# Two convolution layers: a depthwise sum in two halves, later weight splits, and shifted copies spread over three engines

## The chip, the cores and the metric

The kernel runs on one core of one Trainium2 chip. The metric is the device time of one execution in microseconds (us). The engines that matter are TensorE (PE in the profile, with its weight loads as PEld), VectorE (DVE), ScalarE (ACT), GpSimd (POOL) and the queue of SyncE (SP), which issues all the loads. Each engine works through its own instructions strictly in the order of the program, and waits for others at semaphores.

## The reference, cut to what matters

The program is a trunk of four layers on 256 tokens of width 1024. Layers 0 and 3 begin with a convolution mixer, layer 1 with attention, layer 2 with a gated MLP, and each is followed by a channel mixer (ConvFFN). Only the convolution mixer is changed:

```python
def conformer_conv(x, w_in, b_in, w_dw, b_dw, ln_g, ln_b, w_out, b_out):
    h = x @ w_in + b_in                       # 1024 -> 2048
    a, g = jnp.split(h, 2, axis=-1)
    h = a * jax.nn.sigmoid(g)
    h = causal_dwconv(h, w_dw, b_dw)          # 31 taps along the tokens, per channel
    h = jax.nn.silu(layer_norm(h, ln_g, ln_b))
    return h @ w_out + b_out
```

## The kernel before, in words

All matmuls that need accuracy are made of three: a float32 weight tile `raw` is split into a rounded part `whi` (ACT, L87) and the remainder `wlo` (DVE, L88), and so are the activations (`xT_h`, `xT_l`); L105 to L107 add high by high, high by low and low by high.

The 1024 channels of a convolution are worked in four pairs `pr` of two 128-channel halves `n`. For each pair there are these steps:

- `project(pr)`: the input projection of the pair, 96 matmuls of 256 columns into two PSUM banks.
- `glu`: a sigmoid of the gate on ACT (`sg`, L429), and on DVE the gated product `hp` (named `chp`, L430).
- `copies` inside `glu`: 16 copies, each of a block of 32 partitions of `hp` into `h4`, shifted by s tokens, so that four taps can be multiplied at once. Those of ACT are on L422, those of DVE on L424. Pairs 0 to 2 copy both halves at once (32 x 512); pair 3 copies each half by itself (32 x 256). POOL only clears the borders (L411, L413).
- `diagonals(pr)`: the tap weights as small diagonal blocks `dg` (DVE, L404).
- `rest(pr)`: the taps that don't fill a group of four, into `cv`: one on ACT (L446), the others on DVE (L448).
- `taps(pr)`: the groups of four taps as matmuls on PE (L461), then one DVE addition into `cv` (L464).
- `to_tokens(pr, t)`: transposes of `cv` to token-major PSUM banks `tm` (L469), from which `stats` (L475) and `normalise` (L478) make the layer norm. `turn_z` (L483) turns the result back, `activate` (L490, L101, L102) applies the SiLU, and `proj_rows` multiplies with the output weights `wout`, which come in four units `q` of two row blocks.

The order on PE is that in which the code is written. The order on the other engines is fixed when the program is built. The pools have four buffers each for `raw`, `whi`, `wlo` and for the ordinary PSUM banks (`mm`), two for `h4` and three for `hp` and `cv`. So `h4` of pair 2 uses the buffer of pair 0 again, and that of pair 3 the one of pair 1.

The layer's steps stand in the order of this code:

Of the kernel before, what the change touches and what calls it, by code (L numbers as in the profile page):

```python
# [12 lines left out]
AF = mybir.ActivationFunctionType  # L13
# [3 lines left out]
P = 128  # L17
D = 1024
T = 256
# [5 lines left out]
PAD = KW - 1  # L25
# [2 lines left out]
ALPHA = (2 * DEPTH) ** 0.25  # L28
EPS = 1e-5


GROUPS = ((6, 6, 7, 7), (6, 6, 6, 7))
ACT_COPIES = ((11, 16, 12, 9), (7, 15, 13, 8))
GMIN, GMAX = min(map(min, GROUPS)), max(map(max, GROUPS))


@with_exitstack
def trunk(ctx: ExitStack, tc: tile.TileContext, ins, out):
    nc = tc.nc
    pe, dve, act, pool = nc.tensor, nc.vector, nc.scalar, nc.gpsimd  # L40
# [16 lines left out]
    def bank():  # L57
        return mmp.tile([P, 512], F32, name="mm", tag="mm")

    def acc_bank(t, h):  # L60
        return accp.tile([P, 512], F32, name=f"acc{t}{h}", tag=f"acc{t}{h}")

    def accs():
        return [[acc_bank(t, h) for h in range(2)] for t in range(2)]

    order = {}
# [30 lines left out]
    def unit_rows(w, k0, parts=1):  # L97
        return halves(load(w[k0 * P:(k0 + 2) * P, :].rearrange("(k p) n -> p k n", p=P), 2, D), 2, D, parts)
# [264 lines left out]
    def conv(j, prm, lv, turn, nxt, w_first):  # L363


        with tc.tile_pool(name=f"conv{j}", bufs=2) as p:
            wout = ins["a_w_out"][j]
# [40 lines left out]
            def glu(pr, bks):  # L408

                hp = p.tile([P, 2, PAD + T], F32, name="chp", tag="chp", bufs=3)  # L410
                pool.memset(hp[:, :, 0:PAD], 0.0)  # L411
                h4 = p.tile([P, 2, 4, PAD + T], F32, name="h4", tag="h4")
                pool.memset(h4[:, :, :, 0:PAD], 0.0)  # L413
                last = {}

                def copies(a, b):
                    for r in range(4):
                        for s in range(4):
                            src, dst = hp[32 * r:32 * r + 32, a:b, PAD:], h4[32 * s:32 * s + 32, a:b, r, PAD - s:PAD - s + T]
                            i = 4 * r + s  # L420
                            if i * ACT_COPIES[j][pr] // 16 != (i + 1) * ACT_COPIES[j][pr] // 16:
                                last["act"] = act.activation(out=dst, in_=src, func=AF.Identity).ins  # L422
                            else:
                                last["dve"] = dve.tensor_copy(dst, src).ins  # L424

                for n in range(2):
                    c = 2 * pr + n
                    sg = p.tile([P, T], F32, name="sg", tag="sg")
                    act.activation(out=sg, in_=bks[n][:, :T], func=AF.Sigmoid, bias=b_in[:, 8 + c:9 + c])  # L429
                    dve.scalar_tensor_tensor(out=hp[:, n, PAD:], in0=bks[n][:, T:], scalar=b_in[:, c:c + 1], in1=sg, op0=ALU.add, op1=ALU.mult)  # L430
                    if pr == 3:
                        copies(n, n + 1)
                if pr < 3:
                    copies(0, 2)
                return hp, h4, last
# [14 lines left out]

            def taps(pr, t0=0, t1=T, ns=(0, 1)):
                if (pr, t0) not in sums:
                    sums[pr, t0] = bank().rearrange("p (n t) -> p n t", n=2)
                ps = sums[pr, t0][:, :, 0:t1 - t0]
                for n in ns:
                    for g in reversed(range(GROUPS[j][pr])):

                        first_g = g == GROUPS[j][pr] - 1
                        a = t0 if first_g else max(t0, PAD - 4 * g - 3)
                        for r in range(4):  # L460
                            pe.matmul(out=ps[32 * r:32 * r + 32, n, a - t0:], lhsT=dg[pr][:, 4 * n + r, g, :], rhs=h4[pr][:, n, r, 4 * g + a:4 * g + t1],  # L461
                                      start=first_g, stop=g == 0)
                y = cv[pr][:, ns[0]:ns[-1] + 1, t0:t1]
                dve.tensor_tensor(out=y, in0=ps[:, ns[0]:ns[-1] + 1, :], in1=y, op=ALU.add)  # L464
# [7 lines left out]

            def stats(t, h):
                with tc.issue_after(order["dve"]):
                    dve.bn_stats(out=st[t][:, h, :], in_=tm[t][h])  # L475

            def normalise(t, h, mv, rs):
                dve.tensor_scalar(out=z[t][:, h * 512:(h + 1) * 512], in0=tm[t][h], scalar1=mv[:, 0:1], scalar2=rs, op0=ALU.subtract, op1=ALU.mult)  # L478
# [19 lines left out]
            hp[0], h4[0], _ = glu(0, b0)  # L498
            cv[0] = rest(0, hp[0])
            b = project(1)  # L500
            tm = accs()
            dg[1] = diagonals(1)
            hp[1], h4[1], _ = glu(1, b)
            cv[1] = rest(1, hp[1])
            taps(0)
            b = project(2)
            for t in range(2):
                to_tokens(0, t)
            lv = lv()
            nxt = nxt()  # L510
            dg[2] = diagonals(2)
            hp[2], h4[2], _ = glu(2, b)
            taps(1)
            b = project(3)
            for t in range(2):
                to_tokens(1, t)
            dg[3] = diagonals(3)
            ws = [unit_rows(wout, 2 * q) for q in range(2)]
            hp[3], h4[3], last = glu(3, b)
            order.update(last)  # L520
            cv[2] = rest(2, hp[2])
            cv[3] = rest(3, hp[3])
            taps(2, 0, P)
            taps(2, P, T, (0,))
            for t in range(2):
                stats(t, 0)
            nxt = nxt()
            to_tokens(2, 0)
            taps(3, 0, P)
# [388 lines left out]
```

## Time and profile before

| | |
|---|---|
| time, median of 3 runs | 1332.46 us (1331.25 to 1336.53) |
| time of the profiled execution | 1332.35 us |
| its span | 1330.4 us |
| PE busy | 1297.1 us, 97% of the span |
| DVE busy | 1038.2 us, 78% |
| ACT busy | 782.2 us, 59% |
| POOL busy | 56.0 us, 4% |

The span is the time from the first to the last instruction in the trace; the other 1.95 us of the time lie around it. The two convolutions take up about the first 121 us of the span and the stretch from 1027 to 1135 us. A busy share of PE near 100% means that there is always a matmul under way, not that the array works at its peak.

### The profile page before, as it was taken

Reading aid. Unit: us, or ns where it says so; the run is one execution under the profiler, and the core shown is the slowest. Engines: PE = TensorE matmul, PEld = TensorE weight load, DVE = VectorE, ACT = ScalarE, POOL = GpSimd, SP = SyncE. Lnnn points to the kernel's source line nnn. Section 1 sums busy time; section 2 is a strip of 40 time slices with the busy share of each in tenths; the row PEclk is TensorE's granted clock in tenths of the full one; section 3 lists DMA queues with packets and bytes.
Section 4 is the critical chain, followed back from the end, with each engine's and each line's share of the span. In section 5 each row is a group of like instructions: output and inputs, shape, how many; then the busy total and the mean of one; then the engine's idle time right before and its main releaser. Section 6 shows DMA issues by size and latency. Waiting matters only on the chain.

```text
span 1330.4 us, 21217 instructions
## 1 busy us (share of the span) xinstructions
PE 1297.1 (97%) x8338; PEld 1111.3 (84%) x8338; DVE 1038.2 (78%) x1539; ACT 782.2 (59%) x1138; POOL 56.0 (4%) x251
## 2 busy tenths in 40 slices
PE   8979999999999999999999999999999989999997
PEld 8768888886997988886788888988888977988886
DVE  4968987776686987776779665997777986987776
ACT  4973766653674766662555443676662873666661
POOL 0000000001011000100000000000000000000000
PEclk9989999999999999999999999999999999999999
DMA  7713955553732765553867553665553732665530
GB/s 255 258 48 113 296 193 187 186 182 108 245 121 79 256 205 189 192 190 119 314 221 260 166 191 127 220 216 187 187 190 95 238 128 65 220 216 192 189 134 32
DMA packets 167937, 239.79 MB, mean 180 GB/s; under 512 B 7253, under 2 KB 135838, under 8 KB 167838
## 3 DMA queue, kind: packets, MB, share of 16 engines
q1 hardware_dynamic: 167838, 238.44, 54.2%
q8 instruction: 65, 1.06, 0.3%
q14 instruction: 34, 0.28, 0.1%
HBM read 237.38 MB, written 1.05 MB: 179 GB/s over the span
## 4 chain that ended last, share of the span: by engine, by line
PE 90%; ACT 3%; DVE 3%; DMA 1%; issue 1%; SPq 1%; POOL 0%; DVEq 0%; ACTq 0%; POOLq 0%
PE mm L224 26%; PE mm L225 13%; PE acc L107 9%; PE acc L105 9%; PE acc L106 9%; PE mm L107 5%; PE mm L105 4%; PE mm L106 4%; PE mm L232 4%; ACT h L422 2%; PE mm L461 2%; PE mm L242 2%; PE mm L823 1%; DVE cv L448 1%; PE acc L642 1%
## 5 line engine op out<-in xcount | busy, mean ns | idle before, releaser
L88 DVE TENSOR_TENSOR wlo<-raw,whi 128x2048 fp32r<-128x2048 f32 (+2 forms) x239 | 450.0, 1891 | 128.6 <-ACT whi L87 128.1
L224 PE MATMUL mm<-xT_s,whi 128*128 128x512 f32 x1472 | 516.6, 395 | 0.0
L87 ACT ACTIVATE whi<-raw 128x2048 fp32r<-128x2048 f32 (+2 forms) x239 | 377.3, 1593 | 138.2 <-PE mm L224 77.7
L225 PE MATMUL mm<-xT_s,wlo 128*128 128x256 f32 x1472 | 412.3, 280 | 0.0
L224 PEld LDWEIGHTS mm<-xT_s,whi 128*128 128x128 f32 x1472 | 275.9, 187 | 64.1
L225 PEld LDWEIGHTS mm<-xT_s,wlo 128*128 128x128 f32 x1472 | 277.9, 189 | 1.6
L286 DVE SCALAR_TENSOR_TENSOR y<-hp,prm,y 128x256 f32<-128x256 f32 x352 | 164.6, 479 | 32.2 <-ACT y L281 26.1
L281 ACT ACTIVATE y<-hp,prm 128x256 f32<-128x256 f32 x160 | 94.3, 593 | 109.8 <-DVE hp L280 109.3
L105 PE MATMUL acc<-whi,hh 128*128 128x512 f32 x352 | 139.6, 397 | 0.0
L107 PE MATMUL acc<-whi,hl 128*128 128x512 f32 x352 | 139.5, 396 | 0.0
L106 PE MATMUL acc<-wlo,hh 128*128 128x512 f32 x352 | 139.1, 395 | 0.0
L105 PE MATMUL mm<-xT_s,whi 128*128 128x256 f32 x360 | 103.9, 289 | 0.0
L107 PE MATMUL mm<-xT_s,wlo 128*128 128x256 f32 x360 | 101.9, 283 | 0.0
L106 PE MATMUL mm<-xT_s,whi 128*128 128x256 f32 x360 | 101.8, 283 | 0.0
L279 ACT ACTIVATE hp<-mm,prm 128x256 f32<-128x256 f32 x160 | 74.1, 464 | 13.4 <-PE mm L225 13.4
L107 PEld LDWEIGHTS acc<-whi,hl 128*128 128x128 f32 x352 | 66.1, 188 | 17.3 <-DVE hl L102 1.5
L105 PEld LDWEIGHTS acc<-whi,hh 128*128 128x128 f32 x352 | 66.1, 188 | 15.8
L106 PEld LDWEIGHTS acc<-wlo,hh 128*128 128x128 f32 x352 | 66.1, 188 | 14.2
L232 PE MATMUL mm<-xT,raw 128*128 128x128 f32 x608 | 71.1, 277 | 0.4 <-DMA raw<-in_a_w_in_dram 0.4
L232 PEld LDWEIGHTS mm<-xT,raw 128*128 128x128 f32 x608 | 70.3, 194 | 1.2 <-issue 0.8
L105 PEld LDWEIGHTS mm<-xT_s,whi 128*128 128x128 f32 x360 | 69.0, 192 | 1.6 <-issue 1.5
L107 PEld LDWEIGHTS mm<-xT_s,wlo 128*128 128x128 f32 x360 | 69.0, 192 | 0.2 <-DVE wlo L88 0.2
(162 smaller groups left out, 1665.4 us busy)
## 6 DMA issues: line engine op xcount, KB each, us to landing
raw<-in_f_w_up_dram SPq DMA_DIRECT2D x88, 1024.0 KB
raw<-in_f_w_down_dram SPq DMA_DIRECT2D x44, 1024.0 KB
raw<-in_c_w_in_dram SPq DMA_DIRECT2D x24, 1024.0 KB
raw<-in_a_w_in_dram SPq DMA_DIRECT2D x12, 1024.0 KB
raw<-in_b_w_qkv_dram SPq DMA_DIRECT2D x12, 1024.0 KB
raw<-in_c_w_out_dram SPq DMA_DIRECT2D x12, 1024.0 KB
raw<-in_a_w_out_dram SPq DMA_DIRECT2D x8, 1024.0 KB
raw<-in_b_w_o_dram SPq DMA_DIRECT2D x4, 1024.0 KB
```

What stands on the lines that cost most here:

```text
L87: act.activation(out=h, in_=r, func=AF.Identity)
L88: dve.tensor_tensor(out=l, in0=r, in1=h.bitcast(F32), op=ALU.subtract)
L105: pe.matmul(out=ps, lhsT=lh, rhs=rh, start=start, stop=False)
L106: pe.matmul(out=ps, lhsT=lh, rhs=rl, start=False, stop=False)
L107: pe.matmul(out=ps, lhsT=ll, rhs=rh, start=False, stop=stop)
L224: pe.matmul(out=ps, lhsT=wh[:, k, n * P:(n + 1) * P], rhs=xT_hl[:, :, k, :], start=k == 0, stop=False)
L225: pe.matmul(out=ps[:, :T], lhsT=wl[:, k, n * P:(n + 1) * P], rhs=xT_h[:, :, k, :], start=False, stop=k == KT - 1)
L232: pe.matmul(out=ps[:, t * P:(t + 1) * P], lhsT=w[:, k, n * P:(n + 1) * P], rhs=xT[:, t, k, :], start=k == 0, stop=k == KT - 1)
L242: pe.matmul(out=ps, lhsT=xT[:, t, k, :], rhs=ws[k // 4][:, k % 4, :], start=k == 0, stop=k == KT - 1)
L279: act.activation(out=hp[:, 2:], in_=ps[:, T:], func=AF.Identity, bias=b_up[:, c:c + 1])
L281: act.activation(out=yy, in_=hp[:, 2:].rearrange("p (t n) -> p t n", t=2), func=AF.Identity, scale=w2[:, c:c + 1], bias=b_dw[:, c:c + 1])
L286: dve.scalar_tensor_tensor(out=yy, in0=hp[:, d:d + T].rearrange("p (t n) -> p t n", t=2), scalar=w_[:, c:c + 1], in1=yy, op0=ALU.mult, op1 ...
```

## The change

The 16 copies of a pair go to engines by a string of letters, one for each copy: A for ACT, V for DVE, G for POOL. Pairs 0 to 2 have 9 on ACT, 5 on POOL and 2 on DVE; pair 3, with two sets of 16, has 12, 10 and 10. Before, ACT had 11, 16, 12 and 18 in layer 0 and 7, 15, 13 and 16 in layer 3, DVE the rest, and POOL none.

The taps of pairs 0 and 1 are split: the half n=0 stands ahead of the next pair's projection, the half n=1 behind it, directly ahead of the transposes. Their sums go to two accumulator banks (`acc01`, `acc11`) in place of ordinary banks, and the token-major banks of the second half (`tm[t][1]`) are taken later. `rest(2)` moves ahead of `glu(3)`. The first two units of `wout` are loaded where they were, and split into `whi` and `wlo` only behind the first statistics.

```diff
-ACT_COPIES = ((11, 16, 12, 9), (7, 15, 13, 8))
+COPIES = ("AGAGAAVAGAGAAVAG", "AGAGAAVAGAGAAVAG", "AGAGAAVAGAGAAVAG", "AGVAGVAGVAGVAGVA")
...
-                            if i * ACT_COPIES[j][pr] // 16 != (i + 1) * ACT_COPIES[j][pr] // 16:
-                                last["act"] = act.activation(out=dst, in_=src, func=AF.Identity).ins
-                            else:
-                                last["dve"] = dve.tensor_copy(dst, src).ins
+                    for i, who in enumerate(COPIES[pr]):
+                        r, s = i // 4, i % 4
...
+                        if who == "A":
+                            last["act"] = act.activation(out=dst, in_=src, func=AF.Identity).ins
+                        elif who == "V":
+                            last["dve"] = dve.tensor_copy(dst, src).ins
+                        else:
+                            pool.tensor_copy(dst, src)
...
-                    sums[pr, t0] = bank().rearrange("p (n t) -> p n t", n=2)
+                    sums[pr, t0] = (acc_bank(pr, 1) if pr < 2 else bank()).rearrange("p (n t) -> p n t", n=2)
...
-            tm = accs()
+            tm = [[acc_bank(t, 0), None] for t in range(2)]
...
-            taps(0)
+            taps(0, ns=(0,))
             b = project(2)
+            taps(0, ns=(1,))
             for t in range(2):
                 to_tokens(0, t)
...
-            taps(1)
+            taps(1, ns=(0,))
             b = project(3)
+            raws = [load(wout[2 * q * P:(2 * q + 2) * P, :].rearrange("(k p) n -> p k n", p=P), 2, D) for q in range(2)]
+            cv[2] = rest(2, hp[2])
+            taps(1, ns=(1,))
             for t in range(2):
                 to_tokens(1, t)
             dg[3] = diagonals(3)
-            ws = [unit_rows(wout, 2 * q) for q in range(2)]
             hp[3], h4[3], last = glu(3, b)
             order.update(last)
-            cv[2] = rest(2, hp[2])
             cv[3] = rest(3, hp[3])
+            for t in range(2):
+                tm[t][1] = acc_bank(t, 1)
             taps(2, 0, P)
             taps(2, P, T, (0,))
             for t in range(2):
-                stats(t, 0)
+                order["dve"] = stats(t, 0)
+            ws = [halves(raw, 2, D) for raw in raws]
             nxt = nxt()
```

What this does to the order is best seen at three places of layer 0. The line numbers of the changed kernel are up to 6 higher (L449 is L448, L465 is L464 and so on).

**PE, around the first transposes.** `h_231` is `h4` of pair 0 and `h_406` or `h_404` that of pair 1; `acc_398` and its neighbour are the token-major banks. Before, the last matmuls of `project(2)` stand ahead of `to_tokens(0)`:

```order
L106 MATMUL mm<-xT_s,whi 128x256
L107 MATMUL mm<-xT_s,wlo 128x256
L469 MATMUL acc_398<-ident,cv 128x128 x2
L469 MATMUL acc_400<-ident,cv 128x128 x2
L461 MATMUL mm<-h_406,dg 32x256 x4
```

Now the second half of `taps(0)` does:

```order
L462 MATMUL acc_443<-h_231,dg 32x233 x4
L462 MATMUL acc_443<-h_231,dg 32x229 x4
L470 MATMUL acc_398<-ident,cv 128x128 x2
L470 MATMUL acc_399<-ident,cv 128x128 x2
L462 MATMUL acc_656<-h_404,dg 32x256 x4
```

The transposes read `cv`, and so wait for the DVE addition of the taps just ahead of them.

**DVE, around that addition.** `cv_255` is `cv` of pair 0, `cv_428` or `cv_430` that of pair 1, `cv_796` that of pair 2, and `wlo_714` and `wlo_718` (now `wlo_689` and `wlo_693`) are the weight remainders for `project(3)`. Before:

```order
L448 SCALAR_TENSOR_TENSOR cv_430<-chp_404,cprm_203,cv_430 128x256
L178 SCALAR_TENSOR_TENSOR xa1_88<-xa1_88,nb_609 128x1024
L448 SCALAR_TENSOR_TENSOR cv_430<-chp_404,cprm_203,cv_430 128x256
L88 TENSOR_TENSOR wlo_714<-raw_707,whi_713 128x2048
L448 SCALAR_TENSOR_TENSOR cv_430<-chp_404,cprm_203,cv_430 128x256
L464 TENSOR_TENSOR cv_255<-mm_445,cv_255 128x512
```

Now, from the first of these remainders on:

```order
L88 TENSOR_TENSOR wlo_689<-raw_682,whi_688 128x2048
L449 SCALAR_TENSOR_TENSOR cv_428<-chp_402,cprm_203,cv_428 128x256 x5
L431 SCALAR_TENSOR_TENSOR chp_630<-mm_473,cprm_203,sg_634 128x256
L449 SCALAR_TENSOR_TENSOR cv_428<-chp_402,cprm_203,cv_428 128x256 x2
L88 TENSOR_TENSOR wlo_693<-raw_684,whi_692 128x2048
L449 SCALAR_TENSOR_TENSOR cv_428<-chp_402,cprm_203,cv_428 128x256
L449 SCALAR_TENSOR_TENSOR cv_796<-chp_630,cprm_203,cv_796 128x256
L449 SCALAR_TENSOR_TENSOR cv_428<-chp_402,cprm_203,cv_428 128x256
L431 SCALAR_TENSOR_TENSOR chp_630<-mm_474,cprm_203,sg_637 128x256
L449 SCALAR_TENSOR_TENSOR cv_796<-chp_630,cprm_203,cv_796 128x256 x3
L465 TENSOR_TENSOR cv_255<-acc01_443,cv_255 128x256
```

The last part of the addition for pair 0 now stands behind both remainders and both gated products of pair 2.

**DVE, from the copies of pair 3 to the addition of its first taps.** `cv_877` or `cv_796` is `cv` of pair 2, `cv_884` or `cv_876` that of pair 3, and `wlo_976` and `wlo_980` are the remainders of the first two units of `wout`. Before:

```order
L430 SCALAR_TENSOR_TENSOR chp_835<-mm_712,cprm_203,sg_858 128x256
L424 COPY h4_837<-chp_835 32x256 x7
L475 BN_STATS bnst_225<-acc00_398 128x6
L475 BN_STATS bnst_226<-acc10_400 128x6
L464 TENSOR_TENSOR cv_877<-mm_891,cv_877 128x2x128
L448 SCALAR_TENSOR_TENSOR cv_884<-chp_835,cprm_203,cv_884 128x256 x2
L464 TENSOR_TENSOR cv_877<-mm_949,cv_877 128x128
L133 COPY prm_981<-mm_982 128x220
L263 TENSOR_TENSOR prm_981<-prm_981 128x44
L264 TENSOR_TENSOR prm_981<-prm_981 128x44
L464 TENSOR_TENSOR cv_884<-mm_993,cv_884 128x2x128
```

Now:

```order
L404 TENSOR_TENSOR dg_832<-ident4_80,cprm_203 128x1792
L423 COPY h4_836<-chp_834 32x256 x10
L476 BN_STATS bnst_225<-acc00_398 128x6
L465 TENSOR_TENSOR cv_796<-mm_885,cv_796 128x2x128
L476 BN_STATS bnst_226<-acc10_399 128x6
L88 TENSOR_TENSOR wlo_976<-raw_792,whi_975 128x2048
L465 TENSOR_TENSOR cv_796<-mm_943,cv_796 128x128
L88 TENSOR_TENSOR wlo_980<-raw_794,whi_979 128x2048
L133 COPY prm_983<-mm_984 128x220
L465 TENSOR_TENSOR cv_876<-mm_995,cv_876 128x2x128
```

The two remainders came from ahead of pair 2's copies, and now lie between the two additions on which the transposes of pairs 2 and 3 depend.

## Rows read from the trace of the kernel before

**Rows 1.** The page, busy time of the engines (us, share, instructions).

```profile
PE 1297.1 (97%) x8338; PEld 1111.3 (84%) x8338; DVE 1038.2 (78%) x1539; ACT 782.2 (59%) x1138; POOL 56.0 (4%) x251
```

**Rows 2.** Waits of PE: us in total, times, longest.

```profile
PE acc L469 <- ACT h L422: 6.0, 1, 6.0
PE acc L469 <- DVE cv L464: 5.9, 1, 5.9
```

**Rows 3.** Timeline of PE, layer 0: start, us, what, count.

```profile
38.43 5.05 PE L461 MATMUL mm<-h,dg 128*32 128x256 f32 x90 [1.31 <-ACT h L422]
...
55.03 0.60 PE L469 MATMUL acc<-ident,cv 128*128 128x128 f32 x4
...
72.70 4.46 PE L461 MATMUL mm<-h,dg 128*32 128x128 f32 x168
...
84.22 5.94 PE L461 MATMUL mm<-h,dg 128*32 128x128 f32 x168
...
96.41 0.50 PE L105 MATMUL mm<-whi,xT_s 128*128 128x512 f32 x1
```

**Rows 4.** Timeline of PE, layer 3.

```profile
1052.94 5.07 PE L461 MATMUL mm<-h,dg 128*32 128x256 f32 x96
...
1109.94 0.50 PE L105 MATMUL mm<-whi,xT_s 128*128 128x512 f32 x1
```

**Rows 5.** A stretch of layer 0: busy by engine, then PEclk, DMA share, GB/s.

```profile
83.60:86.00 2.40, 2.40 (x39) 2.03 (x42) 1.69 (x6) 2.40 (x3) 0.00 (x0) 0.50 0.03 7
```

**Rows 6.** ACT by form: busy us, mean ns, idle before.

```profile
L87 ACT ACTIVATE whi<-raw 128x2048 fp32r<-128x2048 f32 x178 | 339.7, 1913 | 120.0 <-PE mm L224 77.7 <-PE acc L107 21.0 <-PE mm L107 10.1
...
L422 ACT ACTIVATE h<-chp 32x512 f32<-32x512 f32 x74 | 46.7, 631 | 5.3 <-DVE chp L430 4.2
```

**Rows 7.** DVE by form.

```profile
L88 DVE TENSOR_TENSOR wlo<-raw,whi 128x2048 fp32r<-128x2048 f32 x178 | 407.2, 2289 | 107.8 <-ACT whi L87 107.6
...
L178 DVE SCALAR_TENSOR_TENSOR xa<-xa,nb 128x1024 f32<-128x1024 f32 x14 | 17.0, 1215 | 0.0
...
L424 DVE COPY h<-chp 32x512 f32<-32x512 f32 x22 | 9.2, 416 | 0.3
...
L424 DVE COPY h<-chp 32x256 f32<-32x256 f32 x30 | 8.5, 284 | 0.5
...
L404 DVE TENSOR_TENSOR dg<-ident,cprm 128x1792 f32<-128x1792 f32 x3 | 6.0, 2016 | 0.0
```

**Rows 8.** Timeline of DVE, layer 0.

```profile
39.04 2.07 DVE L448 SCALAR_TENSOR_TENSOR cv<-chp,cprm,cv 128x256 f32<-128x256 f32 x5 [0.83 <-ACT cv L446]
...
44.41 0.47 DVE L430 SCALAR_TENSOR_TENSOR chp<-mm,cprm,sg 128x256 f32<-128x256 f32 x1
...
49.73 0.68 DVE L464 TENSOR_TENSOR cv<-mm,cv 128x512 f32<-128x512 f32 x1
```

**Rows 9.** Timeline of DVE, layer 3.

```profile
1055.89 0.47 DVE L430 SCALAR_TENSOR_TENSOR chp<-mm,cprm,sg 128x256 f32<-128x256 f32 x1
...
1057.41 2.27 DVE L88 TENSOR_TENSOR wlo<-raw,whi 128x2048 fp32r<-128x2048 f32 x1
```

**Rows 10.** POOL by form, the whole span.

```profile
L613 POOL MEMSET qz<- 128x512 f32 x4 | 2.0, 526 | 0.0
...
L53 POOL COPY ident<-ident 32x32 f32<-32x32 f32 x4 | 0.8, 203 | 0.1
...
L602 POOL MEMSET mask<- 128x256 f32 x1 | 0.3, 311 | 8.8 <-PE acc L107 8.8
L603 POOL TENSOR_SCALAR_AFFINE_SELECT mask<-mask 128x128 f32<-128x128 f32 x1 | 0.3, 294 | 0.0
```

**Rows 11.** Timeline of POOL and DVE in layer 2; every L88 (ns min, median, max).

```profile
533.26 2.34 POOL L751 TENSOR_SCALAR_AFFINE_SELECT wsT<-wsT 128x128 f32<-128x128 f32 x1
...
533.07 2.38 DVE L88 TENSOR_TENSOR wlo<-raw,whi 128x2048 fp32r<-128x2048 f32 x1 [0.38 <-ACT whi L87]
...
L88 DVE TENSOR_TENSOR wlo<-raw,whi x239: 667/2286/2377, 19.2 to 1302.2; 128x2048 fp32r<-128x2048 f32 x88, 128x512 fp32r<-128x512 f32 x28, 128x1024 fp32r<-128x1024 f32 x4
```

More of the change, by code (lines that the diff above doesn't have):

```diff
@@ L416, in copies @@
                 def copies(a, b):
[L417 to L420, printed above, removed]
-                            if i * ACT_COPIES[j][pr] // 16 != (i + 1) * ACT_COPIES[j][pr] // 16:
-                                last["act"] = act.activation(out=dst, in_=src, func=AF.Identity).ins
-                            else:
-                                last["dve"] = dve.tensor_copy(dst, src).ins
+                    for i, who in enumerate(COPIES[pr]):
+                        r, s = i // 4, i % 4
+                        src, dst = hp[32 * r:32 * r + 32, a:b, PAD:], h4[32 * s:32 * s + 32, a:b, r, PAD - s:PAD - s + T]
+                        if who == "A":
[4 more added lines that the diff above has]
+                            pool.tensor_copy(dst, src)
                 for n in range(2):
@@ L474, in stats @@
                 with tc.issue_after(order["dve"]):
-                    dve.bn_stats(out=st[t][:, h, :], in_=tm[t][h])
+                    return dve.bn_stats(out=st[t][:, h, :], in_=tm[t][h]).ins
             def normalise(t, h, mv, rs):
```

## The prediction, made before the changed kernel was run

> **What bounds the kernel now.** I read the page first. PE is busy for 97% of the span, DVE for 78%, and POOL does next to nothing [rows 1]. So the time can change only where PE waits or runs slowly, and I looked for that in PE's waits. Two of about six microseconds stand out, one in each convolution, both at the transposes L469 [rows 2]. The timelines of the two convolutions then gave the places. In layer 0, PE starts the taps of pair 0 at 38.43, after 1.31 of waiting for an ACT copy; they take 5.05, `project(2)` lies between their end (43.48) and the first transposes at 55.03, and the output multiplication begins at 96.41 [rows 3]. In layer 3 the same two ends are 1052.94 and 1109.94 [rows 4]. I measure all gains at those last two starts, since what follows is not changed. The long wait of layer 0 also has an aftermath: in the stretch just behind it the granted clock is 0.50, 1.2 GHz instead of 2.4 [rows 5], and the 168 tap matmuls that took 4.46 before it take 5.94 behind it [rows 3]. The wait costs 6.0 and 1.5 of clock.
>
> The profiled execution took 1332.35, 0.1 below the median, so a difference worked out from it is a difference of the median.
>
> **Copies taken from ACT.** A copy of 32x512 takes ACT 0.63 [rows 6]. Pair 0 of layer 0 has 9 where it had 11. The taps, which waited for the last of them, can start at 38.43 − 2 × 0.645 (the mean and a gap) = 37.1, if the POOL copies are done by then. ACT's later sigmoids, and with them `hp` of pair 1, move by the same 1.3: its second half ends at 44.41 + 0.47 − 1.3 = 43.6 [rows 8]. DVE loses some copies as well: layer 0 had 9 long and 14 short ones, which is 9 × 0.42 + 14 × 0.28 = 7.7, and now has 6 and 10, 5.3; layer 3 had 13 and 16, 10.0, and now also 5.3 [rows 7].
>
> **Taps in halves.** A half costs 5.05 / 2 = 2.5. PE does it from 37.1 to 39.7, `project(2)` until 51.4 (11.55, from 43.48 to 55.03), and the second half until 53.9. The transposes come directly behind, and they wait for DVE's addition. Before, that addition started at 49.73, six microseconds after its taps, and this cost nothing: `project(2)` covered it [rows 3, 8]. Now the cover is gone. By the order, DVE has the following to do between the second `hp` of pair 1 and the last part of this addition: 17 taps of 0.41 (five take 2.07, and they follow each other without a gap [rows 8]), two remainders L88 of 2.2 without their wait, two copies of 0.43, one L178 of 1.14 to 1.2, two `hp` of 0.4, two half additions of 0.36 (0.68 for both [rows 8]), and about 0.3 of waiting: 7.0 + 4.4 + 0.9 + 1.1 + 0.8 + 0.7 + 0.3 = 15.2. It ends at 43.6 + 15.2 = 58.8. **So PE waits 58.8 − 53.9 = 4.9 at the first transposes**, in place of nothing.
>
> Then come 0.6 of transposes, 2.5 of half taps and 11.7 of `project(3)`, which ends near 73.7. It ended at 72.2 before, and the other half of pair 1's taps (2.5) is still to come, but that is not lost: behind it stood the wait of 6.0. The second transposes wait another 0.5.
>
> **Weights split later.** The two `wlo` move from ahead of pair 2's copies to behind the first statistics, 2 × 2.2 on DVE. Ahead of the last waits DVE now has `dg` 1.94 (2.0 in [rows 7]), ten copies of 0.297, statistics, the addition of pair 2, two `wlo` and the addition of pair 3. I laid these out with the same durations. The transposes of pair 2 then wait 0.4 instead of 6.0, those of pair 3 wait 1.7, and the output multiplication starts at 95.3, 1.1 earlier than before. ACT's four `whi` follow each other behind the copies of pair 3, 4 × 1.91 = 7.6 [rows 6]; they end 2 before PE turns `z`, and are hidden. The loads on SP's queue that reuse the two `raw` buffers start later by as much as the splits do; the DMA engines are busy for 0.03 of their time there [rows 5], and I cost this at nothing. If such a load came late after all, PE would wait at the first matmuls of the channel mixer.
>
> In layer 3 the first half of the taps starts where the taps did, 1052.94 [rows 4], since pair 0 had 7 ACT copies and now has 9, but there the `hp` of pair 1 falls behind a 2.27 remainder that followed it [rows 9]: it ends at 1058.4. From there 13.8 of DVE work (the same list without the L178 and the waiting, 7.0 + 0.9 + 4.4 + 0.8 + 0.7) end at 1072.1, and PE, done with the second half at 1052.94 + 2.5 + 11.8 + 2.5 = 1069.8, waits 2.3. The output starts at 1108.3, a gain of 1.6. **Without any cost of the POOL copies the sum is 1332.35 − 1.1 − 1.6 = 1329.7**, or 1331 if the new wait of 4.9 lowers the clock as the wait of 6.0 did.
>
> **Copies on POOL.** The trace has no such copy. The nearest rows are POOL's clearing of 512 columns, 0.526, and of 256, 0.311, or 0.84 ns a column. What reading adds is seen in a copy of 32x32 at 0.203 and in a selection of 128x128 at 0.294 [rows 10], about 0.08 above a clearing of that length by the line through the other two. That gives 0.61 for a long copy and 0.39 for a short one. The lower bounds are the clearings themselves; the upper bound puts all of the selection's extra on each column, 0.88 and 0.49. By 0.61, five end before ACT's nine, so POOL itself is not late.
>
> But it may hold up DVE. In layer 2, a selection that takes 0.29 elsewhere took 2.34 beginning at 533.26, and beside it DVE had an L88 from 533.07 to 535.45; that L88, at 2.377, is the longest of all 239 [rows 11]. So a POOL instruction that reads and a DVE instruction of two inputs appear to take turns. I charge DVE with the reading part of each copy, 0.84 ns × 512 = 0.43 or 0.21. In layer 0 ten long copies fall ahead of the first addition that PE now waits for, 4.3, of which gaps on DVE take up 1.3: +3.0. Ten short ones ahead of the last additions cost 2.1, less 1.0 of slack: +1.1. In layer 3 the same gives +2.7 and +1.3. Bounds: nothing, if the turns are short; and with copies of 0.88 that hold DVE for 0.72, +7.7 and +7.3.
>
> The Trainium skill has a rule that speaks against this part of the change ("SBUF — State Buffer", the section on who interferes with whom): a DVE instruction that reads two inputs from SBUF contends with a GpSimd instruction that reads SBUF, and whichever is issued second waits. The trace agrees with it in the one case named, 2.34 against 0.29. The Trainium skill also gives, in "GPSIMD Engine Reference", the section on elementwise cycle accounting, a best measured one-input rate near 0.77 us for 512 elements; an estimate by it would put the sum between the middle and the upper case.
>
> **The sum.** 1332.35 − 2.7 + 8.1 = 1337.8. The wait at the first transposes would be 4.9 + about 2 = 6.8 in layer 0 and 5.0 in layer 3. The first of these is as long as the wait behind which the clock fell, whose loss of 1.5 is in the old time already; if it falls at the new places instead, nothing is added, and if at both, up to 1.5. I say 1338.5.
>
> **The rivals.** *No contention, or hardly any* (1327 to 1334, by the sum 1329.7 to 1331). Against it stands the one selection; for it, that one case is no proof, and that most of the instructions in question are short.
>
> *Slow POOL copies* (1346 to 1356): 0.88 each and DVE held for 0.72, 1329.7 + 15 = 1345 and the clock on top. Only the upper bound speaks for it.
>
> *The relief of ACT decides* (1318 to 1326), the other side. PE's waits of 6.0 and 5.9 name an ACT copy and a DVE addition as what ended them [rows 2], and ACT is relieved of 12 long and 6 short copies in layer 0 and 8 and 4 in layer 3. If DVE reaches the additions of pairs 0 and 1 before PE is done with the halves, the old waits go with their clock and nothing comes for them: 1.7 + 6.0 + 1.5 in layer 0 and 5.9 + 1.5 in layer 3, less four new handovers of 0.5, 14.6, or 1317.7; two thirds of that is 1322. It decides if the addition of pair 0 is done by 54 instead of 58.8, that is, if DVE has 5 less to do than the order and the rows say. That speaks against it.
>
> **How the numbers follow.** Contention at the reading part 0.42 (1335 to 1342), hardly any 0.28, slow copies 0.12, relief of ACT 0.18. The range from 1322 to 1347 leaves out about half of each of the last two. A change under 0.5%, 6.7 us, is about what a measurement of this kernel can't tell from none. The relief is faster, and a little of the second case, 0.20; slow copies and four tenths of the first case are slower, 0.29; the rest, 0.51, is no change.
>
> **What the new profile would show.** Right: PE's longest waits stand at the transposes of pair 0, released by the DVE addition L465, 5 to 7 long; the waits of 6.0 and 5.9 at the transposes of pair 2 are down to 2 or less; POOL's copies take near 0.61 and 0.39, with some far longer beside an L88; the first half taps start at 37.1; the output multiplication starts at 99.5 in layer 0, and in layer 3 59.4 after the first tap, where that was 57.0. Wrong: no wait at the transposes of pair 0; POOL copies of a whole microsecond, with ACT's copies waited for no more and POOL's in their place; or DVE's taps L449 longer than 0.41 throughout, which would be contention of another kind than turns.

## The result, and the profile after

The changed kernel takes 1342.5 us (median of 6 runs, 1340.7 to 1345.8), the kernel before 1333.1 in the runs beside it: a ratio of 1.0069, with a 95% interval of 1.0053 to 1.0085. It is slower by 9 us, where 6 were forecast. By the prediction's own bound of 6.7 us for no change this is a slowdown, to which it gave 0.29, and 0.51 to no change. Of the runs of all the kernels below one stands apart: one of the four of experiment 6 took 6538 us, and its time and ratio here are of the other three. The profiled execution has a span of 1341.3 in place of 1330.4, 10.9 more.

The page first: PE is busier by 5 us with the same matmuls, POOL by 39 [rows 1].

```profile
PE 1301.9 (97%) x8338; PEld 1112.9 (83%) x8338; DVE 1043.3 (78%) x1523; ACT 765.3 (57%) x1108; POOL 95.2 (7%) x301
```

The waits of PE (total, times, longest). The two of six microseconds have become seven, half as long again in sum, and all name the DVE addition [rows 2].

```profile
PE acc L470 <- DVE cv L465: 17.7, 7, 6.3
```

The timeline of PE in layer 0 [rows 3]: the first half taps, the second half behind `project(2)`, the first transposes and the half taps behind them, then the long passes on either side of the transposes of pair 2, and the output multiplication.

```profile
36.86 2.91 PE L462 MATMUL acc<-h,dg 128*32 128x256 f32 x48
...
52.27 2.64 PE L462 MATMUL acc<-h,dg 128*32 128x256 f32 x48
...
61.47 0.90 PE L470 MATMUL acc<-ident,cv 128*128 128x128 f32 x3 [6.30 <-DVE cv L465]
...
62.30 4.33 PE L462 MATMUL acc<-h,dg 128*32 128x256 f32 x48
...
81.97 4.46 PE L462 MATMUL mm<-h,dg 128*32 128x128 f32 x168
89.09 0.44 PE L470 MATMUL acc<-ident,cv 128*128 128x128 f32 x2 [2.23 <-DVE cv L465]
89.46 6.18 PE L462 MATMUL mm<-h,dg 128*32 128x128 f32 x168
...
101.96 0.50 PE L105 MATMUL mm<-whi,xT_s 128*128 128x512 f32 x1
```

The same in layer 3 [rows 4]:

```profile
1058.53 2.64 PE L462 MATMUL acc<-h,dg 128*32 128x256 f32 x48
...
1080.29 0.90 PE L470 MATMUL acc<-ident,cv 128*128 128x128 f32 x3 [4.59 <-DVE cv L465]
1081.12 5.03 PE L462 MATMUL acc<-h,dg 128*32 128x256 f32 x48
...
1108.01 0.44 PE L470 MATMUL acc<-ident,cv 128*128 128x128 f32 x2 [2.13 <-DVE cv L465]
1108.37 4.30 PE L462 MATMUL mm<-h,dg 128*32 128x128 f32 x160
...
1120.82 0.50 PE L105 MATMUL mm<-whi,xT_s 128*128 128x512 f32 x1
```

So the waits of 6 at the transposes of pair 2 are down to 2.2 and 2.1, and new ones of 6.3 and 4.6 stand at those of pair 0. From 96.41 the output of layer 0 has moved to 101.96, 5.5 later; in layer 3 it comes 62.3 after the first tap in place of 57.0, 5.3 more. The two make up nearly all of the 10.9 of the span. The half taps behind each new wait, 48 matmuls that take 2.64 to 2.91 in the other rows, take 4.33 and 5.03. A wait of 1.76 at the transposes of pair 3 in layer 3 is new as well:

```profile
1114.43 0.88 PE L470 MATMUL acc<-ident,cv 128*128 128x128 f32 x4 [1.76 <-DVE cv L465]
```

The stretches of the two rows of half taps, and of the pass behind the wait of 2.23 (busy times by engine, then PEclk, DMA share, GB/s [rows 5]), show the clock that was granted:

```profile
62.30:66.60 4.30, 4.30 (x50) 2.05 (x49) 2.62 (x3) 3.14 (x5) 2.30 (x2) 0.59 0.10 37
...
89.50:95.60 6.10, 6.10 (x170) 5.90 (x169) 5.68 (x8) 5.32 (x4) 0.00 (x0) 0.72 0.39 137
1081.10:1086.10 5.00, 5.00 (x50) 2.19 (x49) 3.50 (x6) 2.44 (x4) 1.36 (x1) 0.50 0.02 3
```

DVE and POOL by form (busy, mean ns): the taps L449 (480 in the kernel before) and both kinds of copies on DVE [rows 7] are longer on average, and the copies on POOL are new.

```profile
L449 DVE SCALAR_TENSOR_TENSOR cv<-chp,cprm,cv 128x256 f32<-128x256 f32 x72 | 35.7, 521 | 3.8 <-ACT cv L447 3.0
L423 DVE COPY h<-chp 32x256 f32<-32x256 f32 x20 | 8.7, 435 | 0.3
L423 DVE COPY h<-chp 32x512 f32<-32x512 f32 x12 | 8.5, 707 | 0.3
...
L425 POOL COPY h<-chp 32x512 f32<-32x512 f32 x30 | 27.6, 919 | 58.3 <-DVE chp L431 57.1
L425 POOL COPY h<-chp 32x256 f32<-32x256 f32 x20 | 11.5, 575 | 1.1
```

POOL's copies by their spread (ns min, median, max), all 50, and the seven long ones between 31 and 46 us: the longest, 2.57, ran beside an L88, like the selection of [rows 11].

```profile
L425 POOL COPY h<-chp x50: 392/700/2569, 31.2 to 1107.0; 32x512 f32<-32x512 f32 x30, 32x256 f32<-32x256 f32 x20
...
L425 POOL COPY h<-chp x7: 693/717/2569, 31.2 to 45.3; 32x512 f32<-32x512 f32 x7
```

### The profile page after: what moved, and what is told of

Read it like the earlier page. It is cut to its first block, busy times and chain, and to the rows that moved or that the text cites. A ratio compares the mean times of both kernels' runs of the same rounds, so it can differ in the third digit from the quotient of the medians.

```text
span 1341.3 us, 21246 instructions
## 1 busy us (share of the span) xinstructions
PE 1301.9 (97%) x8338; PEld 1112.9 (83%) x8338; DVE 1043.3 (78%) x1523; ACT 765.3 (57%) x1108; POOL 95.2 (7%) x301
## 4 chain that ended last, share of the span: by engine, by line
PE 87%; DVE 8%; issue 1%; DMA 1%; ACT 1%; SPq 1%; POOL 0%; DVEq 0%; ACTq 0%; POOLq 0%
PE mm L224 25%; PE mm L225 13%; PE acc L107 9%; PE acc L105 9%; PE acc L106 9%; PE mm L107 4%; PE mm L105 4%; PE mm L106 4%; PE mm L232 4%; DVE cv L449 2%; DVE wlo L88 2%; PE mm L242 2%; DVE h L423 1%; PE mm L829 1%; PE mm L462 1%
## 5 line engine op out<-in xcount | busy, mean ns | idle before, releaser
L88 DVE TENSOR_TENSOR wlo<-raw,whi 128x2048 fp32r<-128x2048 f32 (+2 forms) x239 | 451.0, 1895 | 126.1 <-ACT whi L87 125.6
```

The lines of the kernel that those rows point to most:

```text
L88: dve.tensor_tensor(out=l, in0=r, in1=h.bitcast(F32), op=ALU.subtract)
```

## The experiments

The table gives all of them: the time, the ratio to runs of the kernel before on the same chip (medians 1332.4 to 1333.2) with its interval, the start of the output multiplication in layer 0, and the stretch from the first tap to it in layer 3.

| kernel | us | ratio | output, layer 0 | stretch, layer 3 |
|---|---|---|---|---|
| before | 1333.1 | | 96.4 | 57.0 |
| the change | 1342.5 | 1.0069 (1.0053 to 1.0085) | 102.0 | 62.3 |
| 1 whole taps | 1328.0 | 0.9968 (0.9955 to 0.9980) | 94.7 | 54.9 |
| 2 old deal of copies | 1341.1 | 1.0069 (1.0056 to 1.0082) | 102.8 | 59.7 |
| 3 new deal alone | 1332.1 | 0.9996 (0.9987 to 1.0005) | 97.4 | 56.8 |
| 4 `rest(2)` moved alone | 1332.9 | 0.9997 (0.9988 to 1.0006) | 96.5 | 57.1 |
| 5 POOL clears, reads nothing | 1335.1 | 1.0020 (1.0010 to 1.0029) | 98.3 | 57.5 |
| 6 waits filled | 1338.8 | 1.0049 (1.0032 to 1.0066) | 100.4 | 59.4 |
| 7 whole taps, early ACT tap | 1321.9 | 0.9922 (0.9907 to 0.9937) | 89.9 | 51.9 |
| 8 late splits alone | 1332.4 | 1.0000 (0.9990 to 1.0009) | 96.9 | 56.8 |
| 9 before, early ACT tap | 1332.5 | 0.9991 (0.9981 to 1.0000) | 93.6 | 59.3 |
| 10 as 7, old deal | 1330.5 | 0.9981 (0.9972 to 0.9991) | 93.3 | 55.7 |
| 11 as 7, early splits | 1329.9 | 0.9972 (0.9961 to 0.9983) | 95.3 | 56.1 |
| 12 the change, early ACT tap | 1342.1 | 1.0065 (1.0048 to 1.0082) | 102.0 | 60.8 |

### 1 and 2: halves or POOL

Experiment 1 undoes the halves and nothing else.

```diff
-            taps(0, ns=(0,))
+            taps(0)
             b = project(2)
-            taps(0, ns=(1,))
...
-            taps(1, ns=(0,))
+            taps(1)
             b = project(3)
...
-            taps(1, ns=(1,))
```

> The changed kernel with the taps of pairs 0 and 1 whole again, ahead of the next projection; copies, late weight splits and all else as changed. Theory (the additions of pairs 0 and 1 lost their cover): the waits of 6.3 and 4.6 us at the first transposes vanish with the low clock behind them (4.33 and 5.03 us instead of 2.53 for half taps and whole taps), and little comes back: faster than the kernel before by 7 to 13 us, about 1322. Rival (the POOL copies cost the time themselves, by holding up DVE on the path): still 1338 to 1343.

Measured 1328.0, 14.5 less than with the halves and 5 less than before. The first transposes wait for nothing. The waits at the transposes of pair 2 are 4.84 and 3.78, longer than with the halves, which is why less came back than the 11 I put in the middle. The main claim holds, the size was too hopeful.

Experiment 2 keeps the halves and gives POOL's copies back: the deal of letters is, for each layer and pair, that of the kernel before.

> The changed kernel with the copies dealt out to ACT and DVE as before, none on POOL; halves and late splits stay. Theory: the halves lose their cover with or without POOL, so a wait of about 4 us stays at the first transposes of each convolution, and only the 3 us or so by which POOL holds up DVE ahead of it go: 1331 to 1338. Rival (the copies on POOL are all of the loss): 1328 or less. Rival (contention is nothing, the halves are all): 1341 or more.

Measured 1341.1, beyond the theory and at the edge of the rival that calls contention nothing. The timelines of ACT and DVE show why this is no clean test of contention (three lines further down in this kernel: L450 is ACT's first tap of a half, L424 its copies, L452 the taps on DVE).

```profile
45.81 10.31 ACT L424 ACTIVATE h<-chp 32x512 f32<-32x512 f32 x16 [0.56 <-DVE chp L434]
56.15 0.60 ACT L450 ACTIVATE cv<-chp,cprm 128x256 f32<-128x256 f32 x1
...
56.78 0.48 DVE L452 SCALAR_TENSOR_TENSOR cv<-chp,cprm,cv 128x256 f32<-128x256 f32 x1 [4.32 <-ACT cv L450]
```

ACT's one tap of pair 1 stands behind its 16 copies, and DVE waits 4.32 for it with the rest of its queue, so the addition of pair 0 is late for another reason: the first transposes wait 5.6 there. Contention needed a test in which the order stays.

### 3, 4 and 8: single parts of the change

Experiment 3 has the new strings of letters in the kernel before; experiment 4 moves `cv[2] = rest(2, hp[2])` ahead of `glu(3, b)` in it; experiment 8 loads the first two units of `wout` there as before and splits them behind the first statistics:

```diff
-            ws = [unit_rows(wout, 2 * q) for q in range(2)]
+            raws = [load(wout[2 * q * P:(2 * q + 2) * P, :].rearrange("(k p) n -> p k n", p=P), 2, D) for q in range(2)]
...
             for t in range(2):
-                stats(t, 0)
+                order["dve"] = stats(t, 0)
+            ws = [halves(raw, 2, D) for raw in raws]
```

> The kernel before with the new deal of copies alone (9 ACT, 5 POOL, 2 DVE; pair 3 12, 10, 10). Theory: DVE's copies lengthen to about 0.7 and 0.43 us as in the changed kernel, but the additions are covered by the projections, and ACT's 2.6 us less of short copies shorten the waits of 6.0 and 5.9 us at the transposes of pair 2: 1325 to 1331. Rival (the POOL copies cost the time themselves): 1338 or more.

> The kernel before with one step moved: the tail taps of pair 2 ahead of the copies of pair 3, as the change has it. In the kernel before ACT's one tap of pair 2 stands behind its 18 copies of pair 3, and the transposes wait for it. Theory: this one move takes away most of the waits of 6.0 and 5.9 us and the low clock behind the first: 1317 to 1326. Rival (the copies of pair 3 or DVE's remainders are late anyway and take the wait's place): 1329 to 1333.

> The kernel before with the splits of the first two units of the output weights behind the first statistics, and nothing else. Theory (this is the part of the change that pays: the second gated product of pair 2, and with it all copies of pairs 2 and 3, no longer stand behind two remainders of 2.3 us): the waits of 6.0 and 5.9 us shorten by 2 to 4 each, less 1 us each for the remainders where they now stand: 1326 to 1330. Rival (the copies of pair 3 on ACT set the wait): 1332 or more.

Measured 1332.1, 1332.9 and 1332.4: no difference in any of them, and the theory was wrong three times, by 1 us in the first, 7 in the second and 2 in the last; the rivals named for experiments 4 and 8 came true. In experiment 3 the waits at the transposes of pair 2 are 6.5 and 5.3: DVE's copies are longer, much as in the change, and ACT's are fewer. That one pays for the other is my reading; no run parts the two. In experiment 4 the wait is 6.0 as before. ACT's tap of pair 2 was in fact ahead of the copies of pair 3 already, since the order on the engines is not that of the code; the row in the waits of before that named an ACT copy was read too literally. In the kernel before, two chains end together where the transposes start at 83.60, the last copies of pair 3 on ACT at 83.55 and the addition of pair 2 on DVE at 83.54, and the taps of pair 3 behind the transposes need those copies. So an earlier addition alone can gain no more than the 0.7 of the transposes, and earlier copies alone nothing:

```profile
79.69 3.86 ACT L422 ACTIVATE h<-chp 32x256 f32<-32x256 f32 x9 [1.10 <-DVE chp L430]
...
83.12 0.42 DVE L464 TENSOR_TENSOR cv<-mm,cv 128x256 f32<-128x256 f32 x1
```

In experiment 8 the wait is shorter in layer 0, 4.2, but 1.5 of waiting appears at the transposes of pair 3.

### 5: contention by itself

```diff
-                            pool.tensor_copy(dst, src)
+                            pool.memset(dst, 0.0)
```

> The changed kernel with each POOL copy turned into a clearing of the same target, so that POOL writes but reads nothing; those parts of the convolution's sum are then left out of what is computed. The rows of DVE and ACT stand in the same order. Theory (taking turns with POOL's reads holds up DVE ahead of additions that PE waits for): DVE's copies are back to 0.42 and 0.29 us, the waits of 6.3 and 4.6 us shorten by 2 to 3 each, the later ones by 1 each: 1334 to 1337. Rival (contention hardly matters, as the 1341.1 of the deal without POOL may say): 1340 or more.

Measured 1335.1, 7.4 less than the change; the theory's 1334 to 1337 holds. By form on DVE (busy, mean ns) in this kernel:

```profile
L449 DVE SCALAR_TENSOR_TENSOR cv<-chp,cprm,cv 128x256 f32<-128x256 f32 x72 | 33.0, 481 | 5.5 <-ACT cv L447 4.7
L423 DVE COPY h<-chp 32x256 f32<-32x256 f32 x20 | 6.8, 338 | 0.3
L423 DVE COPY h<-chp 32x512 f32<-32x512 f32 x12 | 5.0, 420 | 0.3
```

DVE's long copies are back from 707 to 420 ns and the taps from 521 to 481; the first transposes wait 4.1 and 2.0 in place of 6.3 and 4.6:

```profile
59.03 0.90 PE L470 MATMUL acc<-ident,cv 128*128 128x128 f32 x3 [4.14 <-DVE cv L465]
...
1074.31 0.76 PE L470 MATMUL acc<-ident,cv 128*128 128x128 f32 x3 [2.01 <-DVE cv L465]
```

The edit takes more away than POOL's reads: a clearing also waits for no gated product, and so comes at another time. The contention goes away in two ways here. The clearings of pairs 0 and 1 wait for nothing, and in layer 0 come in the first nine microseconds, when DVE has none of these instructions. Those of pair 2 lie beside DVE's taps, which they leave at 0.41 from one to the next. Only the short copies of pair 3 stay longer than the 284 of before. The timeline of POOL and the spread of these DVE copies, beside the ten clearings of pair 3 and behind them, fit this:

```profile
79.35 3.55 POOL L425 MEMSET h<- 32x256 f32 x10
...
L423 DVE COPY h<-chp x2: 386/388/389, 82.3 to 82.7; 32x256 f32<-32x256 f32 x2
...
L423 DVE COPY h<-chp x2: 286/288/290, 84.3 to 84.6; 32x256 f32<-32x256 f32 x2
```

The clearings end at 82.9; beside them a copy takes 388, behind them 288. So in these rows POOL holds up DVE's copies even when it only writes, and DVE's instructions of two inputs not then. The rule cited in the prediction from the Trainium skill ("SBUF — State Buffer", who interferes with whom) says the latter, and the same section has the former for DVE's faster copy modes. The trace agrees with the latter, the taps at 0.41; for the former it shows the longer copies, but no row shows the mode in which they ran.

### 6: the clock by itself

The waits are filled with matmuls that repeat the first half taps of pair 1 into the bank that the real ones overwrite.

```diff
             taps(0, ns=(1,))
+            fill(1, 1 if j else 2)
             for t in range(2):
                 to_tokens(0, t)
```

> The changed kernel with matmuls that repeat the first half taps of pair 1 (into the bank that the real ones overwrite) in the waits at the first transposes: twice in layer 0, about 5.1 us, once in layer 3, 2.5 us. DVE and ACT keep their order. Theory (the clock falls because PE idles): the half taps behind the wait in layer 0 take 2.5 us in place of 4.3, and the taps behind the one in layer 3 up to 2.5 us less, while the transposes start where they did: 1337.5 to 1340.5. Rival (the low clock has another cause than the wait): 1342 or more, with the same slow taps.

Measured 1338.8, 3.7 less than the change, with 144 matmuls more. The timeline of PE, layer 0 and layer 3 (L474 is the fill, L480 the transposes), and the two stretches by engine and clock:

```profile
55.45 5.05 PE L474 MATMUL acc<-h,dg 128*32 128x256 f32 x96
...
62.18 0.55 PE L480 MATMUL acc<-ident,cv 128*128 128x128 f32 x3 [1.42 <-DVE cv L465]
62.65 2.64 PE L462 MATMUL acc<-h,dg 128*32 128x256 f32 x48
...
1079.00 2.64 PE L462 MATMUL acc<-h,dg 128*32 128x256 f32 x48
```

```profile
62.70:65.20 2.50, 2.50 (x49) 1.42 (x48) 2.47 (x3) 2.42 (x5) 2.44 (x2) 1.00 0.33 129
1079.00:1081.60 2.60, 2.60 (x50) 1.48 (x49) 2.54 (x4) 2.53 (x5) 1.70 (x1) 1.00 0.00 0
```

The transposes start no earlier for it, but the half taps behind them run at the full 2.4 GHz and take 2.64 in place of 4.33 and 5.03, 4.1 less in sum.

### 7: the chain behind the rest of the waits

In experiment 1 the transposes of pair 2 still wait 4.84. Its timelines of PE, ACT and DVE show a chain that leads there (L447 is ACT's first tap of a half, L421 its copies, L449 the taps on DVE, L431 the gated product):

```profile
81.27 0.69 PE L470 MATMUL acc<-ident,cv 128*128 128x128 f32 x2 [4.84 <-DVE cv L465]
...
62.12 5.82 ACT L421 ACTIVATE h<-chp 32x512 f32<-32x512 f32 x9 [3.61 <-DVE chp L431]
67.97 0.60 ACT L447 ACTIVATE cv<-chp,cprm 128x256 f32<-128x256 f32 x1
...
68.60 0.48 DVE L449 SCALAR_TENSOR_TENSOR cv<-chp,cprm,cv 128x256 f32<-128x256 f32 x1 [4.58 <-ACT cv L447]
...
71.34 0.47 DVE L431 SCALAR_TENSOR_TENSOR chp<-mm,cprm,sg 128x256 f32<-128x256 f32 x1
```

DVE waits 4.58 for ACT's tap of pair 2, which stands behind nine copies, and the first gated product of pair 3 is queued behind that on DVE. Experiment 7 writes ACT's tap directly behind the gated product of its half:

```diff
                     dve.scalar_tensor_tensor(out=hp[:, n, PAD:], in0=bks[n][:, T:], scalar=b_in[:, c:c + 1], in1=sg, op0=ALU.add, op1=ALU.mult)
+                    k0 = 4 * GROUPS[j][pr]
+                    act.activation(out=cv[pr][:, n, :], in_=hp[:, n, k0:k0 + T], func=AF.Identity, scale=w_rest[:, (k0 - 4 * GMIN) * 8 + c:(k0 - 4 * GMIN) * 8 + c + 1], bias=b_dw[:, c:c + 1])
                     if pr == 3:
```

> The kernel with whole taps (1328.0), and besides ACT's one tap of each half written directly behind its gated product, ahead of the copies. In that kernel DVE reaches the gated product of pair 3 only 4.6 us late, because a tap of pair 2 waits for ACT's tap, which stands behind nine copies. Theory (that chain is the wait of 4.8 and 3.8 us left at the transposes of pair 2): these waits fall below 1.5 us, with the low clock behind them: 1316 to 1322. Rival (the copies of pair 3 themselves or the late remainders are the limit): 1326 to 1330.

Measured 1321.9, 10.5 less than the kernel before on the same chip (1332.4). The timelines of DVE (the gated product) and of PE, at the place where the wait was:

```profile
68.42 0.48 DVE L432 SCALAR_TENSOR_TENSOR chp<-mm,cprm,sg 128x256 f32<-128x256 f32 x1 [1.59 <-ACT sg L431]
```

```profile
77.64 0.44 PE L469 MATMUL acc<-ident,cv 128*128 128x128 f32 x2 [1.02 <-DVE cv L464]
78.01 4.46 PE L461 MATMUL mm<-h,dg 128*32 128x128 f32 x168
...
1086.05 0.44 PE L469 MATMUL acc<-ident,cv 128*128 128x128 f32 x2 [1.10 <-DVE cv L464]
```

The gated product comes 2.9 earlier, and now waits 1.59 for ACT's sigmoid, which still stands behind the nine copies. The waits are 1.0 and 1.1, and the 168 matmuls behind the first take 4.46 where the kernel before needed 5.94 [rows 3].

### 9 to 12: what the fastest kernel needs

Experiment 9 puts the early ACT tap, and `rest(2)` ahead of `glu(3)`, into the kernel before. Experiments 10 and 11 are experiment 7 with the old deal of copies, and with the splits back where they were. Experiment 12 is the change, halves and all, with the early ACT tap.

> The kernel before with ACT's one tap of each half directly behind its gated product, and the tail taps of pair 2 ahead of the copies of pair 3; copies on ACT and DVE and splits as before. Theory (the wait at the transposes of pair 2 has three links, each of which has to go: ACT's late tap, the remainders ahead of the second gated product of pair 2, and ACT's 12 and 9 copies): the other two stay and hold most of the wait: 1326 to 1332. Rival (the late tap alone sets it): 1319 to 1323.

> The fastest kernel so far (whole taps, early ACT taps, late splits; 1321.9) with the copies dealt to ACT and DVE as before, none on POOL. Theory (with the additions covered, POOL's copies are a gain, since ACT's copies of pairs 2 and 3 come in series ahead of the transposes: 12 in place of 9 long ones and 9 in place of 6 short ones twice): 2 to 4 us more in each convolution, 1325 to 1330. Rival (POOL's reads cost as much on DVE as they save on ACT): 1321 to 1323.

> The fastest kernel so far with the splits of the first two units of the output weights back ahead of the copies of pair 2. Theory: two remainders of 2.3 us stand ahead of the second gated product of pair 2 again, so pair 2's copies and all behind them are 4.6 us later, 1 us of which is made up at the waits behind the late splits: 1325 to 1330. Rival (the late splits don't matter, as by themselves they made no difference): 1321 to 1323.

> The changed kernel, halves and all, with ACT's one tap of each half directly behind its gated product: against the fastest kernel (1321.9) only the halves differ. Theory (the halves take the cover from the additions, and hold the copies of pair 3 back until the second half has freed their buffer): the addition of pair 0 still stands behind the work of pairs 1 and 2 on DVE, so the waits at the first transposes stay at 3 to 6 us and those of pairs 2 and 3 near 2: 1335 to 1342. Rival (the late tap on ACT was what made the additions late): 1321 to 1330.

Measured 1332.5, 1330.5, 1329.9 and 1342.1. Only experiment 11 lies inside the range of its theory; the others are 0.1 to 0.5 above theirs, and in experiments 9 and 10 for a reason that it did not name. In 9 the waits at the transposes of pair 2 do fall, to 2.1 and 2.5, and the output of layer 0 comes 2.8 earlier; so the other two links hold less there than I said. Layer 3 loses it again, 59.3 in place of 57.0: the second remainder for `project(2)` comes late, behind the taps of pair 1 and the addition of pair 0 on DVE. The timelines of PE in experiments 9 and 10:

```profile
1061.28 0.58 PE L107 MATMUL mm<-xT_s,wlo 128*128 128x256 f32 x1 [3.00 <-DVE wlo L88]
```

```profile
1061.22 0.39 PE L110 MATMUL mm<-xT_s,wlo 128*128 128x256 f32 x1 [3.00 <-DVE wlo L91]
```

The stretches of `project(2)` behind these two waits (busy times by engine, then PEclk, DMA share, GB/s), experiment 9 and then 10:

```profile
1061.30:1066.00 4.70, 4.70 (x22) 4.70 (x23) 3.80 (x2) 2.66 (x5) 0.00 (x0) 0.50 0.63 223
```

```profile
1061.30:1066.00 4.70, 4.70 (x40) 4.70 (x40) 4.70 (x4) 3.55 (x7) 0.00 (x0) 1.00 0.61 223
```

Experiment 9 has the low clock behind the wait, 22 matmuls where experiment 10 does 40, and its next transposes stand 2.5 later behind the wait, 11.0 in place of 8.5. So in layer 3 wait and clock lose 5.5, and the shorter wait at the transposes of pair 2 gives 3.4. The profiled execution of experiment 10 is the fastest of its ten, 1327.8, so its trace shows less than the median loses.

In 11 the waits at the transposes of pair 2 are back at 4.8 and 4.2, as the theory has it. In 12 the waits at the first transposes are 6.4 and 4.5 and those of pair 2 2.2 and 2.1, much the same as in the change: the halves cost 1342.1 − 1321.9 = 20 there, with everything else equal in the code.

## Why the prediction was right, and where it was off

**Taps in halves.** The step that decided it was right. It put the wait at the first transposes at 4.9 in layer 0 and 2.3 in layer 3 without contention; experiment 5 shows 4.1 and 2.0. With contention it had 6.8 and 5.0; the change shows 6.3 and 4.6, by the addition L465 as named. Undoing the halves takes 14.5 off, and with the early ACT tap as well 20. The cover of `project(2)` is what the change gives away. The halves cost in a second way, which the prediction does not name. The copies of pair 3 go into the buffer of pair 1, which is free only when the second half of its taps is done:

```profile
80.97 5.22 ACT L421 ACTIVATE h<-chp 32x256 f32<-32x256 f32 x12 [0.91 <-PE acc L462]
```

In the change the first gated product of pair 3 is done at 73.7 in layer 0 and its copies start at 81.0; in experiment 7 they start at 69.0. How the 20 divide between the two ways no run shows; the waits at the first transposes in experiment 12 are 10.9 of them, without the clock behind.

**Contention.** The term was 8.1, and experiment 5 measures 7.4 in the time and 8.2 in the span (1341.3 to 1333.1). That the numbers meet so closely is in part luck. The waits at the transposes of pairs 0 and 2 shorten by 6.7 in sum; most of the rest is the clock behind the wait of pair 2 in layer 0, where the 168 matmuls take 4.5 in place of 6.2, less a new wait of 0.9 at the transposes of pair 3. The one selection of 2.34 beside an L88 [rows 11] had pointed at a part of the mechanism: on DVE's way to the addition of pair 0 in layer 0, from 31 us on, instructions of two inputs take 1.9 more than in experiment 5, the L88 beside POOL 2.69 in place of 2.28, but four of DVE's own copies take 1.2 more, which the prediction did not charge. The sign of another kind of contention, taps longer throughout, did not come: their median is 480 ns, the longest 833. Contention costs this much because the addition is on the path now; in experiment 3, where a projection covers it, the same copies on POOL together with the relief of ACT change nothing that can be measured. Of the two prices for a copy the short one was right: the shortest 32x256 copy took 0.392 against 0.39. The long one was low: the shortest of those before 46 us took 0.693 against 0.61, though still below the 0.77 that the prediction cites.

**The clock.** This is the term that was mis-sized. The prediction added 0.7, as half of a loss of 1.5 that might only change its place, and put 1.5 as the most. The two rows of half taps lose 1.7 and 2.4, and the second of these, behind the wait forecast as 5.0 in layer 3, it did not count. The low clock now stands behind the new waits in both convolutions, and behind the wait of 2.23 in layer 0 as well, where it was before. In layer 3 the pass behind the transposes of pair 2 had 0.73 before and has the full clock now, but the time is waited out at those of pair 3, 1.76: in experiments 6 and 12 that pass is slow again, and that wait is gone. Experiment 6 takes away the part behind the first transposes alone: 3.7 in the time, 4.1 in the two rows of taps. By the layout the output should have started at 99.5 in layer 0, and the stretch of layer 3 should have been 59.4; they are 102.0 and 62.3, and with the waits filled 100.4 and 59.4. So 4.5 of the 5.3 that were missing in the two stretches were this.

**Late splits and the waits of pair 2.** The waits did go down, from 6.0 and 5.9 to 2.2 and 2.1, where 2 or less was forecast with contention. The price, a wait of 1.7 at the transposes of pair 3, came in layer 3 (1.76), and in layer 0 the slower pass covers it. But the gain is no property of the late splits alone: by themselves they change nothing (experiment 8), and neither does `rest(2)` (experiment 4) or the new deal (experiment 3). With the taps whole the three together give 5.

**The rival that the relief of ACT decides** did not come about in the change. Its mechanism is real, though: with the halves undone and ACT's tap early, the kernel is 10.5 faster than before, and without the new deal or without the late splits about 8 or 7 of this are lost, by the ratios, since the chips differ (experiments 10 and 11; in the trace of the former 3 are the late remainder in layer 3). What kept it from showing was, by the prediction's condition, the addition of pair 0, done at 61.4 where the prediction had put the turning point at 54.

## What to carry to other kernels

Before a wait is cut in two by moving half of a producer behind the work that covered it, look at what else stands in the queue of the engine that finishes it: here the addition had 17 us of other work ahead of it from the gated product of pair 1 on (44.4 to 61.0 in layer 0), and the projection was hiding that. Look also at the buffers that the moved half holds for longer. In experiment 1 DVE waited 4.58 for one small result of ACT, with the rest of its queue behind it, so a short instruction that another engine needs belongs ahead of a run of copies. With the cover kept this took 1328.0 down to 1321.9; in the kernel before and in the change it gave nothing (experiments 9 and 12), where other waits took its place. When two chains end together, relieving one shows no gain, and single tests of the parts mislead. Price a new wait of several microseconds on TensorE together with the slower matmuls behind it.

## What the runs showed of the hardware that was not expected

The clock did not follow the length of the wait alone. Behind waits of nearly the same length the granted clock of the next long pass was 0.72 (after 2.23, in layer 0) and full in layer 3 (after 2.13: 160 matmuls in 4.30); in experiment 6 it was low behind both (2.21 and 2.12), and in experiment 12 it was 0.72 behind both (2.21 and 2.12). The clearest case is experiments 9 and 10: 0.50 and 1.00 behind waits of 3.00 at the same place of `project(2)`. What ran before them differs, and these runs, one traced execution of each kernel, don't settle which part of it counts.

A clearing on POOL, which reads nothing, lengthens a DVE copy of 32x256 from 288 to 388 ns beside it (experiment 5). The prediction had charged DVE for POOL's reads alone; by their length the copies on DVE are the instructions that suffered most, 707 against 416 for the long ones.
